# Sink's logit as one more score column in sliding-window attention: one maximum over four heads, negation on ScalarE

## The chip, the cores and the metric

The kernel runs on one core of one Trainium2 chip. Its time is the device time of one execution in microseconds (us). Five engines work side by side, each through its own queue in order: PE (TensorE, matmuls and transposes), DVE (VectorE), ACT (ScalarE), POOL (GpSimd) and SP, which only issues DMAs. "Span" is the time from the first to the last instruction of the profiled execution. Lines such as L1671 are lines of the kernel before; the change shifts what lies behind it (L1671 becomes L1674, L1681 to L1685 become one less or vanish, the later lines are one less).

## The reference

Two transformer blocks run one after the other in fp32: a first block with causal differential attention, stick-breaking attention, cross attention and an MLP, and a second block with sliding-window attention, RWKV and gated linear attention. The change touches only the sliding-window attention. Eight query heads share two key heads (four each), a block has 128 queries, its keys are its own 128 and the 128 before, and each head has a sink: a learned logit that takes part in the softmax and has no value row.

```python
s = jnp.einsum('bnqhgd,bnkhd->bnhgqk', qb, kb) * (D ** -0.5)
s = s - slopes[...] * dist
s = jnp.where(valid[None, :, None, None], s, -jnp.inf)
sink = jnp.broadcast_to(sinks.reshape(Hkv, G)[:, :, None, None], s.shape[:-1] + (1,))
p = jax.nn.softmax(jnp.concatenate([s, sink], axis=-1), axis=-1)[..., :-1]
o = jnp.einsum('bnhgqk,bnkhd->bnqhgd', p, vb)
```

## The kernel before

The sequence of 1024 is worked in two halves of 512 (c = 0 and 1). A weight matmul in fp32 is three matmuls on operands split into a high and a low half (L208 to L210); ACT makes the high half (L200), DVE or POOL the low one (L201).

The sliding attention runs once for each half, in two stretches of the program, called **window 1** (c = 0, g_window0, about 1925 to 2010 us in the profile) and **window 2** (c = 1, in g_tail, about 2230 to 2300 us). Each has 8 units: 4 blocks of 128 queries by 2 key heads. A unit is four heads and has three stages:

- `a()`: eight score matmuls (L1667, L1668) into two PSUM tiles of two heads; for each tile DVE scales it, adds the bias (L1670) and reduces it to its maximum (L1671); then DVE takes the maximum with the sink (L1673), subtracts it from the sink (L1674) and negates it (L1675); ACT takes exp of the sink's difference (L1676) and of each head's scores with their sum (L1678); DVE adds the two (L1681) and takes the reciprocal (L1682); ACT scales heads 0 and 1 (L1684), POOL heads 2 and 3 (L1685).
- `tr()`: PE transposes the probabilities (L1699), ACT copies them out of PSUM (L1702).
- `pv()`: PE multiplies them with the values (L1709), DVE multiplies with the gate (L1711).

The stages of one unit are issued 0, 2 and 3 units late, so that three units are in flight; the scores' tile `wp` has three buffers. The first two units of window 1 have only 128 keys.

Window 1 is woven with the RWKV preparation (g_p2a: projections on PE, elementwise work L1463 to L1549 on DVE, whose result RK goes to DRAM at L1552 and comes back as rk at L1769). Window 2 is woven with the output projection of the rows done (the matmuls on `ya`) and with the first half's final norm (g_final0: loads hd and zd, DVE L2314 and L2316, POOL L2317, store). Behind window 2 come the remaining output projection on `yw` and the last norm. The order on each engine is set by a scheduler that places instructions by estimated durations, so an edit moves neighbours too.

Of the kernel before, what the change touches and what calls it, by code (L numbers as in the profile page):

```python
# [12 lines left out]
F32 = mybir.dt.float32  # L13
# [3 lines left out]
AF = mybir.ActivationFunctionType  # L17
ALU = mybir.AluOpType
AX = mybir.AxisListType
# [3 lines left out]
P = 128  # L23
# [3 lines left out]
CH = 512  # L27
# [141 lines left out]
class K:  # L169
# [1418 lines left out]
    def win_load(s, mx, c):  # L1588

        nc = s.nc  # L1590
        st = [mx.tile([P, 2, CH], F32, tag="wp", name=s.nm("ws"), bufs=3) for _ in range(3)]
        t = [st[i // 2][:, i % 2, :] for i in range(6)]
        sink = mx.tile([P, 8], F32, name="sink")
        s.nc.sync.dma_start(sink, s.A["sink"])
        kst = [mx.tile([P, P + CH], F32R, name=s.nm("k2")) for _ in range(4)]
        q8 = s.tl(s.xp, [P, KT, CH], "act", F32R)
        if c == 1:
            s.nc.sync.dma_start(t[5][:, :P], s.pd[s.AK * P : (s.AK + 1) * P, c * CH - P : c * CH])
        s.get_rows(t[4], s.pd, s.AK, c)
        for h in range(4):  # L1600
            s.get_rows(t[h], s.pd, s.AQ + h, c)
        yield 0
        if c == 1:
            s.stack_k(mx, t[5][:, :P], [k[:, :P] for k in kst])
        s.stack_k(mx, t[4], [k[:, P:] for k in kst])
        yield 0
        qst = []
        for h in range(4):
            qst.append(s.stack_q(mx, t[h], [q8[:, 2 * h, :], q8[:, 2 * h + 1, :]]))
            yield 0  # L1610
        s.win = mx, sink, kst, qst
# [33 lines left out]
    def w_units(s, wn, c, qst, kst, bias, sink, one):  # L1645

        nc = s.nc
        V = nc.vector
        mm = nc.tensor.matmul
        st = {"n": 0}  # L1650

        def unit(b, g):
            u = {}
            nk = 1 if b == 0 else 2
            w = nk * P
# [2 lines left out]
            ga = slice(64 * g, 64 * g + 64)  # L1658

            def a():  # L1660
                p = u["p"] = wn.tile([P, 4, 2 * P], F32, tag="wp", name=s.nm("wp"), bufs=3)
                t = s.sm.tile([P, 6, 4], F32, tag="wt", name=s.nm("wt"))
                for z in range(2):
                    ps = s.ps([P, 2, 2 * P])
                    for y in range(2):
                        q = qst[2 * z + y][g][:, (b % 4) * P : (b % 4 + 1) * P]
                        mm(ps[:, y, :w], q, kst[g][:, k0 : k0 + w], start=True, stop=False)  # L1667
                        mm(ps[:, y, :w], q, kst[2 + g][:, k0 : k0 + w], start=False, stop=True)  # L1668
                    pz = p[:, 2 * z : 2 * z + 2, :w]
                    V.scalar_tensor_tensor(pz, ps[:, :, :w], 0.125, bs[:, 2 * z : 2 * z + 2, :], ALU.mult, ALU.add)  # L1670
                    V.tensor_reduce(t[:, 0, 2 * z : 2 * z + 2], pz, AX.X, ALU.max)  # L1671
                sk = sink[:, 4 * g : 4 * g + 4]
                V.tensor_tensor(t[:, 1, :], t[:, 0, :], sk, ALU.max)  # L1673
                V.tensor_tensor(t[:, 2, :], sk, t[:, 1, :], ALU.subtract)  # L1674
                V.tensor_scalar(t[:, 1, :], t[:, 1, :], -1.0, None, ALU.mult)  # L1675
                nc.scalar.activation(t[:, 2, :], t[:, 2, :], AF.Exp)  # L1676
                for h in range(4):
                    nc.scalar.activation(  # L1678
                        p[:, h, :w], p[:, h, :w], AF.Exp, bias=t[:, 1, h : h + 1], accum_out=t[:, 3, h : h + 1]
                    )  # L1680
                V.tensor_tensor(t[:, 3, :], t[:, 3, :], t[:, 2, :], ALU.add)  # L1681
                V.reciprocal(t[:, 4, :], t[:, 3, :])  # L1682
                for h in range(2):
                    nc.scalar.activation(p[:, h, :w], p[:, h, :w], AF.Copy, scale=t[:, 4, h : h + 1])  # L1684
# [739 lines left out]
```

## Time and profile before

| | us |
|---|---|
| median of 3 runs (lowest, highest) | 2347.19 (2345.37, 2354.68) |
| the profiled execution | 2346.06 |
| its span | 2344.3 |
| PE busy | 2245.4 (96%) |
| DVE busy | 1292.4 (55%) |
| ACT busy | 1034.7 (44%) |
| POOL busy | 691.2 (29%) |

The profiled execution lasts 1.76 us longer than its span, and lies 1.13 us under the median. The shares are means over the whole program; the two windows take about 155 us of it, and there the shares are others: they are in the rows further down. In the rows a form such as 128x4 is partitions by elements, "x8" is how many instructions, "idle before" what the engine stood still ahead of them and for whom.

### The profile page before, as it was taken

Reading aid. Unit: us, or ns where it says so; the run is one execution under the profiler, and the core shown is the slowest. Engines: PE = TensorE matmul, PEld = TensorE weight load, DVE = VectorE, ACT = ScalarE, POOL = GpSimd, SP = SyncE. Lnnn points to the kernel's source line nnn. Section 1 sums busy time; section 2 is a strip of 40 time slices with the busy share of each in tenths; the row PEclk is TensorE's granted clock in tenths of the full one; section 3 lists DMA queues with packets and bytes.
Section 4 is the critical chain, followed back from the end, with each engine's and each line's share of the span. In section 5 each row is a group of like instructions: output and inputs, shape, how many; then the busy total and the mean of one; then the engine's idle time right before and its main releaser. Section 6 shows DMA issues by size and latency. Waiting matters only on the chain.

```text
span 2344.3 us, 34760 instructions
## 1 busy us (share of the span) xinstructions
PE 2245.4 (96%) x13056; PEld 1898.0 (81%) x13056; DVE 1292.4 (55%) x2312; ACT 1034.7 (44%) x2196; POOL 691.2 (29%) x1035
## 2 busy tenths in 40 slices
PE   8999999999999999999999999999999999989886
PEld 7898999988898888888888888887787776677765
DVE  7665656676754554422423422346846658656485
ACT  6655656674643424411311311344633348434463
POOL 4101100000500003556565650035322333224343
PEclk9999999999999999999999999999998999989898
DMA  4010010123241211222222221133343233533461
GB/s 135 28 42 23 31 39 28 46 77 124 66 140 54 99 37 45 75 79 72 77 83 72 78 74 45 52 124 122 119 134 105 74 127 100 166 126 105 131 208 50
DMA packets 116393, 200.06 MB, mean 85 GB/s; under 512 B 14048, under 2 KB 33792, under 8 KB 115456
## 3 DMA queue, kind: packets, MB, share of 16 engines
q1 hardware_dynamic: 111456, 184.72, 24.1%
q0 software_dynamic: 4768, 13.11, 1.7%
q8 instruction: 102, 1.67, 0.3%
q14 instruction: 67, 0.55, 0.1%
HBM read 163.70 MB, written 34.08 MB: 84 GB/s over the span
## 4 chain that ended last, share of the span: by engine, by line
PE 56%; DVE 8%; DMA 4%; ACT 2%; issue 2%; POOL 1%; SPq 0%; DVEq 0%; ACTq 0%; POOLq 0%
PE ps L208 17%; PE ps L209 16%; PE ps L210 16%; DVE act L1957 1%; DVE itmp L1954 1%; PE ps L1827 1%; PE ps L2124 1%; PE ps L1709 1%; DMA stg<-w2l 0%; PE ps L1785 0%; DVE wh L201 0%; DMA stg<-w2t 0%; PE ps L232 0%; DVE wp L1670 0%; ACT wh L200 0%
## 5 line engine op out<-in xcount | busy, mean ns | idle before, releaser
L208 PE MATMUL ps<-act,wh 128*128 128x512 f32 x1664 | 670.3, 405 | 7.5 <-ACT wh L200 5.7
L210 PE MATMUL ps<-act,wh 128*128 128x512 f32 x1664 | 658.1, 396 | 0.0
L209 PE MATMUL ps<-act,wh 128*128 128x512 f32 x1480 | 584.1, 395 | 2.6 <-DVE act L204 1.6
L200 ACT ACTIVATE wh<-stg 128x512 fp32r<-128x512 f32 x374 | 234.6, 630 | 581.4 <-PE ps L209 463.6
L208 PEld LDWEIGHTS ps<-act,wh 128*128 128x128 f32 x1664 | 318.9, 192 | 79.6 <-issue 6.1
L210 PEld LDWEIGHTS ps<-act,wh 128*128 128x128 f32 x1664 | 318.1, 191 | 68.7 <-issue 0.2
L209 PEld LDWEIGHTS ps<-act,wh 128*128 128x128 f32 x1480 | 282.1, 191 | 60.3 <-DVE act L204 2.4
L201 DVE TENSOR_TENSOR wh<-stg,wh 128x512 fp32r<-128x512 f32 x260 | 198.8, 767 | 154.4 <-ACT wh L200 152.9
L201 POOL TENSOR_TENSOR wh<-stg,wh 128x512 fp32r<-128x512 f32 x114 | 161.4, 1420 | 336.3 <-ACT wh L200 301.6
L907 DVE TENSOR_TENSOR act<-ps,act 128x512 f32<-128x512 f32 x112 | 77.0, 689 | 178.0 <-PE ps L210 177.8
L546 DVE TENSOR_TENSOR_SCAN pw<-pw,zero 128x128 f32<-128x128 f32 (+7 forms) x64 | 86.8, 1358 | 82.9 <-POOL pw L542 78.1
L247 POOL TENSOR_TENSOR nacc<-nacc,t 128x512 f32<-128x512 f32 x28 | 39.0, 1396 | 260.4 <-ACT t L246 256.0
L944 POOL TENSOR_TENSOR ad<-ad,cb 128x256 f32<-128x256 f32 x96 | 72.3, 754 | 146.6 <-DMA ad<-adaT 143.6
L1144 DVE SCALAR_TENSOR_TENSOR t<-ps,Rm 128x512 f32<-128x512 f32 x64 | 44.0, 691 | 127.6 <-PE ps L210 126.9
L949 POOL TENSOR_TENSOR ad<-ad 128x128 f32<-128x128 f32 (+5 forms) x288 | 97.3, 338 | 16.8
L208 PE MATMUL ps<-hid,wh 128*128 128x512 f32 x256 | 101.2, 395 | 0.0
L210 PE MATMUL ps<-hid,wh 128*128 128x512 f32 x256 | 101.1, 395 | 0.0
L209 PE MATMUL ps<-hid,wh 128*128 128x512 f32 x256 | 101.0, 395 | 0.0
L1145 ACT ACTIVATE t<-t 128x512 f32<-128x512 f32 x64 | 40.4, 631 | 135.8 <-DVE t L1144 135.8
L208 PE MATMUL ps<-wh,act 128*128 128x256 f32 x320 | 95.9, 300 | 0.0
L210 PE MATMUL ps<-wh,act 128*128 128x256 f32 x320 | 91.3, 285 | 0.0
L209 PE MATMUL ps<-wh,act 128*128 128x256 f32 x320 | 91.1, 285 | 0.0
(515 smaller groups left out, 4663.8 us busy)
## 6 DMA issues: line engine op xcount, KB each, us to landing
stg<-w2f SPq DMA_DIRECT2D x84, 256.0 KB, 3.1
stg<-w_dn SPq DMA_DIRECT2D x80, 256.0 KB, 2.8
stg<-w_up SPq DMA_DIRECT2D x64, 256.0 KB, 2.8
ad<-adaT POOLq DMA_DIRECT2D x96, 128.0 KB, 2.6
stg<-w2o SPq DMA_DIRECT2D x32, 256.0 KB, 2.7
pd<-t SPq DMA_DIRECT2D x30, 256.0 KB, 2.3
t<-yd SPq DMA_DIRECT2D x26, 256.0 KB, 3.5
rkd<-RK SPq DMA_DIRECT2D x4, 1280.0 KB, 5.7
```

What stands on the lines that cost most here:

```text
L200: nc.scalar.activation(hi, src, AF.Copy)
L201: (eng or nc.vector).tensor_tensor(lo, src, hi.bitcast(F32), ALU.subtract)
L208: mm(out, lh, rh, start=first, stop=False)
L209: mm(out, lh, rl, start=False, stop=False)
L210: mm(out, ll, rh, start=False, stop=last)
L247: nc.gpsimd.tensor_tensor(acc, acc, t[:, :n], ALU.add)
L546: V.tensor_tensor_scan(m[:, :w][:, ::-1], m[:, :w][:, ::-1], s.zero.to_broadcast([P, w]), 1.0, ALU.mult, ALU.add)
L907: s.nc.vector.tensor_tensor(hh, ps, hh, ALU.add)
L944: tt(t, t, cb[:, 256 * y : 256 * y + 256], ALU.mult)
L949: tt(acc[:, n, z, :] if w == 2 else a, a, b, ALU.add)
L1144: V.scalar_tensor_tensor(t, ps, 0.0, R[:, c * CH : (c + 1) * CH], ALU.max, ALU.mult)
L1145: nc.scalar.activation(t, t, AF.Square)
```

## The change

The scores' tile gets one more column for each head (4 x 257 instead of 4 x 256). POOL copies the four sinks into column w (128 x 4 elements) at the start of the unit. One reduction over 4 x (w+1) replaces two over 2 x w, and gives the maximum with the sink in it. ACT negates it. Exp runs over w+1 columns, and its sum holds the sink's term. The maximum with the sink, the subtraction, the negation and the addition on DVE go, and so does the Exp of the sink on ACT. The tiles in which the loads are staged have the same tag and take the new size.

```diff
     def win_load(s, mx, c):
-        st = [mx.tile([P, 2, CH], F32, tag="wp", name=s.nm("ws"), bufs=3) for _ in range(3)]
-        t = [st[i // 2][:, i % 2, :] for i in range(6)]
+        st = [mx.tile([P, 4, 2 * P + 1], F32, tag="wp", name=s.nm("ws"), bufs=3) for _ in range(3)]
+        st = [x.rearrange("p a w -> p (a w)") for x in st]
+        t = [st[i // 2][:, i % 2 * CH : i % 2 * CH + CH] for i in range(6)]
...
             def a():
-                p = u["p"] = wn.tile([P, 4, 2 * P], F32, tag="wp", name=s.nm("wp"), bufs=3)
+                p = u["p"] = wn.tile([P, 4, 2 * P + 1], F32, tag="wp", name=s.nm("wp"), bufs=3)
                 t = s.sm.tile([P, 6, 4], F32, tag="wt", name=s.nm("wt"))
+                nc.gpsimd.tensor_copy(p[:, :, w : w + 1], sink[:, 4 * g : 4 * g + 4, None])
                 for z in range(2):
...
                     V.scalar_tensor_tensor(pz, ps[:, :, :w], 0.125, bs[:, 2 * z : 2 * z + 2, :], ALU.mult, ALU.add)
-                    V.tensor_reduce(t[:, 0, 2 * z : 2 * z + 2], pz, AX.X, ALU.max)
-                sk = sink[:, 4 * g : 4 * g + 4]
-                V.tensor_tensor(t[:, 1, :], t[:, 0, :], sk, ALU.max)
-                V.tensor_tensor(t[:, 2, :], sk, t[:, 1, :], ALU.subtract)
-                V.tensor_scalar(t[:, 1, :], t[:, 1, :], -1.0, None, ALU.mult)
-                nc.scalar.activation(t[:, 2, :], t[:, 2, :], AF.Exp)
+                V.tensor_reduce(t[:, 0, :], p[:, :, : w + 1], AX.X, ALU.max)
+                nc.scalar.activation(t[:, 1, :], t[:, 0, :], AF.Copy, scale=-1.0)
                 for h in range(4):
                     nc.scalar.activation(
-                        p[:, h, :w], p[:, h, :w], AF.Exp, bias=t[:, 1, h : h + 1], accum_out=t[:, 3, h : h + 1]
+                        p[:, h, : w + 1], p[:, h, : w + 1], AF.Exp, bias=t[:, 1, h : h + 1],
+                        accum_out=t[:, 3, h : h + 1],
                     )
-                V.tensor_tensor(t[:, 3, :], t[:, 3, :], t[:, 2, :], ALU.add)
                 V.reciprocal(t[:, 4, :], t[:, 3, :])
```

How it moves instructions is shown at three places, each before and after the change. The first is DVE in window 2, the seventh unit (wp_21241 and wt_21242 before, wp_21185 and wt_21186 after), with the neighbours between its scores and the next unit's; before:

```order
L1670 SCALAR_TENSOR_TENSOR wp_21241<-ps_21243,act_18780 128x512
L1670 SCALAR_TENSOR_TENSOR wp_21241<-ps_21250,act_18780 128x512
L1671 TENSOR_REDUCE wt_21242<-wp_21241 128x2 x2
L1681 TENSOR_TENSOR wt_21160<-wt_21160 128x4
L201 TENSOR_TENSOR yw<-t_3766_21055,yw 128x4x128
L1673 TENSOR_TENSOR wt_21242<-wt_21242,sink 128x4
L1682 RECIPROCAL wt_21160<-wt_21160 128x4
L2316 SCALAR_TENSOR_TENSOR t_3804_21275<-t_3804_21275,GP,zacc 128x512
L1674 TENSOR_TENSOR wt_21242<-sink,wt_21242 128x4
L1675 TENSOR_SCALAR wt_21242<-wt_21242 128x4
```

and after, up to the next unit's scores (wp_21246):

```order
L1673 SCALAR_TENSOR_TENSOR wp_21185<-ps_21194,act_18748 128x2x256
L1674 TENSOR_REDUCE wt_21186<-wp_21185 128x4
L2313 SCALAR_TENSOR_TENSOR t_3805_21222<-t_3805_21222,gv,rst 128x512
L201 TENSOR_TENSOR yw<-t_3766_21007,yw 128x4x128
L1710 SCALAR_TENSOR_TENSOR t_3796_21168<-ps_21230,t_3796_21168 64x512
L1673 SCALAR_TENSOR_TENSOR wp_21246<-ps_21249,act_18748 128x2x256
L1673 SCALAR_TENSOR_TENSOR wp_21246<-ps_21255,act_18748 128x2x256
L1681 RECIPROCAL wt_21186<-wt_21186 128x4
```

Before, four instructions of other work (L1681 and L1682 of the sixth unit, L201, L2316) and three steps of the unit's own stand between its second score tile and the negation that ACT's Exp waits for; after, only the reduction does, and the unit's next DVE instruction is its reciprocal, four to five instructions further on.

The second place is POOL in window 1, around the scaling of units 2 and 3 (wh are low halves of weights); before:

```order
L1685 TENSOR_TENSOR wp_18102<-wp_18102,wt_18103 128x2x128
L201 TENSOR_TENSOR wh_18321<-stg_18318,wh_18320 128x512
L1685 TENSOR_TENSOR wp_18183<-wp_18183,wt_18184 128x512
L201 TENSOR_TENSOR wh_18417<-stg_18414,wh_18416 128x512
L201 TENSOR_TENSOR wh_18423<-stg_18420,wh_18422 128x512
L1685 TENSOR_TENSOR wp_18271<-wp_18271,wt_18272 128x512
```

and after:

```order
L1684 TENSOR_TENSOR wp_18098<-wp_18098,wt_18099 128x2x128
L201 TENSOR_TENSOR wh_18225<-stg_18222,wh_18224 128x512
L1665 COPY wp_18259<-sink 128x4
L201 TENSOR_TENSOR wh_18299<-stg_18296,wh_18298 128x512
L1684 TENSOR_TENSOR wp_18175<-wp_18175,wt_18176 128x2x256
L201 TENSOR_TENSOR wh_18305<-stg_18302,wh_18304 128x512
L1665 COPY wp_18350<-sink 128x4
```

The sink's copy stands among the low halves and the scalings; from the fourth unit of a window on it waits for PE's transposes of the unit that held the tile before, and what stands behind it on POOL waits with it. Here wp_18259 is the fourth unit's tile and wp_18350 the fifth's.

The third place is PE in window 2, ahead of the seventh unit's scores (L208 to L210 are the fill matmuls on ya, L1699 the fifth unit's transposes, L1709 the fourth's values); before:

```order
L209 MATMUL ps_21203<-ya_20717,wh_21132 128x512
L210 MATMUL ps_21203<-ya_20717,wh_21133 128x512
L1709 MATMUL ps_21218<-act_18780,vt 128x512 x2
L1699 MATMUL ps_21226<-ident,wp_21069 128x128
L1699 MATMUL ps_21232<-ident,wp_21069 128x128
L1667 MATMUL ps_21243<-k_3670_20536,act_20540 128x256
L1668 MATMUL ps_21243<-k_3672_20538,act_20540 128x256
```

and after:

```order
L209 MATMUL ps_21147<-ya_20685,wh_21080 128x512
L210 MATMUL ps_21147<-ya_20685,wh_21081 128x512
L1708 MATMUL ps_21162<-act_18748,vt 128x512
L1698 MATMUL ps_21170<-ident,wp_21021 128x128 x2
L1698 MATMUL ps_21176<-ident,wp_21021 128x128 x2
L1670 MATMUL ps_21188<-k_3670_20504,act_20508 128x256
```

The last fill matmul stands ahead of the seventh unit's scores before and after, so that the last two units and the drain behind them have none; after, one of the fourth unit's two value matmuls has moved behind the seventh unit's first scores, and two more transposes ahead of them.

## Rows read from the trace of the kernel before

**Rows 1.** The page: the chain that ended last, shares of the span by engine

```profile
PE 56%; DVE 8%; DMA 4%; ACT 2%; issue 2%; POOL 1%; SPq 0%; DVEq 0%; ACTq 0%; POOLq 0%
```

**Rows 2.** Busy time of each engine and PE's clock, in stretches of both windows

```profile
1935.00:1945.00 10.00, 7.63 (x30) 5.89 (x30) 9.40 (x22) 7.24 (x19) 3.79 (x3) 0.83 0.15 51
1975.00:2005.00 30.00, 24.87 (x103) 16.80 (x103) 21.83 (x42) 21.46 (x55) 9.55 (x7) 0.94 0.41 135
2250.00:2300.00 50.00, 37.50 (x172) 24.64 (x171) 42.12 (x76) 32.40 (x93) 18.17 (x14) 0.97 0.57 189
```

**Rows 3.** What PE waited for in window 1: us in total, times, longest

```profile
PE ps L1699 <- ACT wp L1684: 4.6, 2, 2.4
```

**Rows 4.** What PE waited for in window 2

```profile
PE ps L1709 <- ACT act L1702: 8.5, 6, 3.7
PE ps L1699 <- ACT wp L1684: 3.8, 3, 1.6
```

**Rows 5.** DVE's groups in window 1: busy us, mean ns, idle before

```profile
L1671 DVE TENSOR_REDUCE wt<-wp 128x2 f32<-128x512 f32 x12 | 7.8, 672 | 0.0
...
L1675 DVE TENSOR_SCALAR wt<-wt 128x4 f32<-128x4 f32 x8 | 5.0, 629 | 0.1
...
L1681 DVE TENSOR_TENSOR wt<-wt 128x4 f32<-128x4 f32 x8 | 3.4, 431 | 6.9 <-ACT wp L1678 6.9
L1673 DVE TENSOR_TENSOR wt<-wt,sink 128x4 f32<-128x4 f32 x8 | 3.0, 371 | 0.0
...
L1674 DVE TENSOR_TENSOR wt<-sink,wt 128x4 f32<-128x4 f32 x8 | 2.1, 261 | 0.1
```

**Rows 6.** DVE's groups in window 2

```profile
L1675 DVE TENSOR_SCALAR wt<-wt 128x4 f32<-128x4 f32 x8 | 5.9, 733 | 0.2
L1673 DVE TENSOR_TENSOR wt<-wt,sink 128x4 f32<-128x4 f32 x8 | 4.8, 606 | 0.0
...
L1674 DVE TENSOR_TENSOR wt<-sink,wt 128x4 f32<-128x4 f32 x8 | 3.5, 438 | 0.1
L1681 DVE TENSOR_TENSOR wt<-wt 128x4 f32<-128x4 f32 x8 | 3.2, 405 | 1.8 <-ACT wp L1678 1.8
```

**Rows 7.** ACT's groups in window 1

```profile
L1678 ACT ACTIVATE wp<-wp,wt 128x256 f32<-128x256 f32 x24 | 11.9, 495 | 2.3 <-DVE wt L1675 2.3
...
L1676 ACT ACTIVATE wt<-wt 128x4 f32<-128x4 f32 x8 | 1.6, 202 | 3.5 <-DVE wt L1674 3.5
```

**Rows 8.** ACT's groups in window 2

```profile
L1678 ACT ACTIVATE wp<-wp,wt 128x256 f32<-128x256 f32 x32 | 15.9, 497 | 5.2 <-DVE wt L1675 5.1
...
L1676 ACT ACTIVATE wt<-wt 128x4 f32<-128x4 f32 x8 | 1.6, 199 | 3.9 <-DVE wt L1674 3.9
```

**Rows 9.** DVE in order of time, window 1: start, duration

```profile
1939.02 0.68 DVE L1540 TENSOR_TENSOR RK<-pt,pt 128x512 f32<-128x512 f32 x1
1939.62 1.23 DVE L1673 TENSOR_TENSOR wt<-wt,sink 128x4 f32<-128x4 f32 x1
```

**Rows 10.** POOL at the same time

```profile
1938.39 2.44 POOL L201 TENSOR_TENSOR wh<-stg,wh 128x512 fp32r<-128x512 f32 x1 [4.77 <-ACT wh L200]
```

**Rows 11.** DVE in order of time, window 2

```profile
2266.80 1.52 DVE L2316 SCALAR_TENSOR_TENSOR t<-t,GP,zacc 128x512 f32<-128x512 f32 x1
```

**Rows 12.** POOL's smallest groups, whole span

```profile
L949 POOL TENSOR_TENSOR ad<-ad 128x4 f32<-128x4 f32 x48 | 15.5, 323 | 0.7
...
L537 POOL MEMSET pw<- 128x1 f32 x64 | 6.3, 99 | 119.6 <-PE ps L482 119.4
```

**Rows 13.** POOL's low halves of weights in window 1

```profile
L201 POOL TENSOR_TENSOR wh<-stg,wh 128x512 fp32r<-128x512 f32 x15 | 21.9, 1463 | 47.7 <-ACT wh L200 36.7 <-DMA rk<-rkd 9.7 <-PE ps L1490 1.4
```

**Rows 14.** SP's queue, window 1: the store of RK

```profile
1994.27 0.45 SPq L1552 DMA_DIRECT2D rkd<-RK  x1
```

**Rows 15.** POOL behind the load that follows it

```profile
2008.92 1.26 POOL L201 TENSOR_TENSOR wh<-stg,wh 128x512 fp32r<-128x512 f32 x1 [9.66 <-DMA rk<-rkd]
```

**Rows 16.** The chain in order of time, window 2

```profile
2272.32 3.98 DMA t<-hd
```

## The prediction

> **What bounds the kernel now.** I read the chain that ended last first, and in it its shares by engine [rows 1]: PE holds 56%, DVE 8%, everything else little. The kernel as a whole is a matmul kernel, and an edit of some DVE instructions can only pay where PE stands still for them. So the second view is the busy time of the engines in stretches of the two windows [rows 2]. PE is not full there: it is busy 7.63 of 10 us (1935 to 1945), 24.87 of 30 (1975 to 2005) and 37.50 of 50 (2250 to 2300), so it idles 2.37 + 5.13 = 7.50 us in window 1 and 12.50 us in window 2. DVE is the full engine beside it: 9.40 of 10, and 42.12 of 50; in 1975 to 2005 its 21.83 lie nearly all in the first 20 us, since the RWKV work has ended by then. The third view is the waits of PE: in window 1 its transposes wait 4.6 us for ACT's scaling [rows 3], in window 2 its value matmuls wait 8.5 us for ACT's copy of the transposes, and the transposes 3.8 us for the scaling [rows 4]. ACT is named, but ACT itself waits: before the Exps for DVE's negation, 2.3 us in window 1 and 5.1 in window 2, and before the sink's Exp for the subtraction, 3.5 and 3.9 us [rows 7, 8]. That chain (scores, maximum, three small DVE steps, Exp, addition, reciprocal, scaling, transposes, values) is what the windows are bound by, where the DVE steps stand in a queue with RWKV's or the final norm's work.
>
> **What goes from DVE.** Four instructions of 128x4 in each of 16 units. They should be short, and are not: in window 1 the four groups take 5.0 + 3.4 + 3.0 + 2.1 = 13.5 us [rows 5], in window 2 5.9 + 4.8 + 3.5 + 3.2 = 17.4 us [rows 6], 30.9 us together for 64 instructions. The reason is seen in two rows of the same moment: L1673 starts at 1939.62 and lasts 1.23 us to 1940.85 [rows 9], while POOL works on a low half from 1938.39 for 2.44 us, to 1940.83 [rows 10]. The small instruction ends when POOL's does. The wide L1540 ahead of it kept its 0.68 us [rows 9], and POOL's 2.44 us stand against a mean of 1.463 in its group [rows 13]: there POOL waited. I take it that the two engines hold each other off, so that the small steps are worth their stretched times as long as nothing else takes their place.
>
> **What changes in the reductions.** Two reductions of 128x512 cost 2 x 0.672 = 1.34 us [rows 5]. One over 1028 elements costs 0.672 x 1028 / 512 = 1.35 us if all of it goes by the element, and less by one start if not. A start is not shown by itself; the least stretched group of small steps, L1674 at 0.261 us [rows 5], is an upper bound for it. So the saving is 0 to 0.26 us a unit; I take 0.1, which is 1.6 us over 16 units. On the other side the one reduction begins only after the second score tile, where before the first could begin earlier; since DVE is full it has other work meanwhile, and I cost that at nothing; with DVE empty it would be up to 0.67 us a unit.
>
> **What comes to ACT.** The negation takes the place of the sink's Exp: the same form, 0.20 us [rows 7, 8], one for one. The Exps grow by one column of 256, 0.497 / 256 = 0.002 us each, 64 of them: 0.1 us. That an odd width of 257 costs more than its one element, no row shows; the bound on that side is one more small ACT instruction for each Exp, 64 x 0.20 = 13 us of ACT, half hidden since ACT is busy only 32.40 of 50 and 21.46 of 30 us [rows 2]. I take nothing, as the row it is nearest to is the Exp itself. What counts more is the order: the negation now follows the reduction at once on another engine, so that ACT's waits of 2.3 + 3.5 = 5.8 us in window 1 and 5.1 + 3.9 = 9.0 us in window 2 [rows 7, 8] should largely go.
>
> **What comes to POOL.** One copy of 128x4 a unit. Its cost is between a memset of 128x1 at 0.099 and a two-operand step of 128x4 at 0.323 us [rows 12]; with one operand I take 0.2, which is 1.6 us a window. POOL is busy 9.55 of 30 and 18.17 of 50 us [rows 2], so its time is hidden. Its wait is another thing: the first three copies of a window wait for the loads' staging tiles, the later five for PE's transposes of the unit three before, and behind them in POOL's order are low halves of weights and the scalings of heads 2 and 3. These transposes are issued before the scores that need the tile in any case, so most copies will find the tile free. In return DVE's reduction waits for the copy, and behind that reduction stands everything on DVE. I put 1 us on each window for this.
>
> **The sum.** Window 1: of PE's 7.5 us idle, ACT's 5.8 us of waiting is the part that this chain makes. That it also shortens the program needs what ends the window to come earlier. RK's store is issued at 1994.27 [rows 14], and the low halves that PE's next projections want stand behind the load of rk, for which POOL waits 9.66 us until 2008.92 [rows 15]. RK is made on DVE, which is full up to there, and loses 13.5 us of work less what lies behind 1994; so it comes earlier by about as much as PE's idle allows. I take 5.8 + 0.8 (reductions) - 1 = 5.6 us. Window 2: ACT's 9.0 us, but here the chain runs through the final norm's transfers: hd's load of 3.98 us at 2272.32 [rows 16], into a tile that an output store has to leave first. A faster DVE meets that load sooner and then waits for it, with all that is queued behind L2314. I take half of 9.0, and again 0.8 - 1: 4.3, say 4 us. Together 9.6, rounded down to 9 us since some of the moved neighbours will fall badly. The profiled execution would go from 2346.06 to 2337; it lies 1.13 us under the median, so the median goes from 2347.19 to **2338**. The bounds: nothing at all from window 2 and half of window 1 gives 3 us; both windows with ACT's whole waits give 14.8. So 2332 to 2344 is the forecast's own range.
>
> A rule of the Trainium skill speaks against counting the stretched times. SBUF — State Buffer, section "SBUF: two separate sides", says that VectorE and GpSimd share one pair of ports under an exclusive lock: a VectorE instruction with two operands in SBUF (or in a two-port mode) and a GpSimd instruction exclude each other for their whole length, and whichever starts first wins. The trace agrees with the exclusion (1.23 us for L1673 [rows 9]). By this rule the stretch isn't a property of the small steps: the next DVE instruction that needs the pair inherits it. That is the second rival.
>
> **Rivals.**
> First, all of the idle time goes: DVE was the sole bound, and PE fills its 7.50 and 12.50 us. For it: PE at a mean granted clock of 0.83 in 1935 to 1945 [rows 2], a mixture of its levels of 1.2 and 2.4 GHz in a stretch in which it stood still, so that a stall also costs speed behind it. Against it: the last two units of window 2 have no fill matmuls in either order, and idle time there is the latency of the chain. 2347 - 20 = 2327.
>
> Second, the stretches are handed on. L2316 took 1.52 us at 2266.80 [rows 11], a wide two-operand step with POOL at work: so wide steps can be stretched too. Then the gain is the small steps' own time, at most 64 x 0.261 = 16.7 instead of 30.9 us, and the sum shrinks in proportion to 9 x 16.7 / 30.9 = 4.9 us; the copies, at most 16 x 0.323 = 5.2 us of POOL, stretch others in turn and take about half of that. Against it: in window 1 most instructions that follow the small ones read PSUM or are reductions. About -2 us, 2345.
>
> Third, slower: the copy at the head of POOL's queue. The place is the five later units of each window, ten copies; the price is a DVE queue that stands at its reduction until POOL has come past a low half whose high half ACT has not made. POOL waited 36.7 us for ACT ahead of 15 low halves [rows 13], 2.4 us each; ten times that is 24 us. Less the 9 us won it is +15 us, 2362. It decides from the fourth such wait on (4 x 2.4 exceeds the 9 us). For it: the copies stand between low halves in POOL's new order. Against it: the copies can run as soon as the tile is free, which is a unit ahead of the reduction.
>
> **Chances and range.** Forecast 0.50, all idle gone 0.15, handed on 0.24, slower through POOL 0.11. A measurement of this kernel can tell about 0.5% from no change, 11.7 us. Faster by more than that is the first rival, 0.15, and the forecast's far end, 0.13: 0.28. Slower by more is most of the third, 0.08. Within is the rest, 0.64. The range of 8 in 10 goes from 2328, which takes in most of the first rival, to 2350, which takes in the handing-on and an extra wait or two, and leaves out the third.
>
> **What would show it.** Right: DVE's busy time falls by some 30 us in the two windows, ACT's waits ahead of the Exps shrink to under 1 us a window, and PE's idle in the three stretches falls from 20.0 to about 11 us, with nothing moved elsewhere. The handing-on would show as longer means of L2314, L2316, L201 and RWKV's two-operand steps; the load as a DVE wait for hd well over what it is now; the third rival as DVE's reduction waiting for POOL's copy. The forecast is wrong if the windows end when they did although DVE has less to do, or if a wait of DVE for POOL of several us stands in them.

## The result and the profile after

The changed kernel took 2336.29 us (median of 12 runs, 2329.39 to 2343.58) against 2351.80 us for the kernel before (12 runs, 2345.37 to 2357.62): a ratio of 0.9939, 95% interval 0.9923 to 0.9955, so 14.3 us faster (10.6 to 18.1) by the ratio. The forecast was 9 us faster, 2338 us. The profiled execution took 2335.09 us with a span of 2333.3 us, 11.0 us less than before.

Where did the 11.0 us of this pair go? I cut both traces at the same instructions: window 1 from its first score matmul to the first transpose of rk behind its last scores, window 2 from its first score matmul to the end of its last value matmul.

| stretch | before, us | after, us |
|---|---|---|
| ahead of window 1 | 1922.6 | 1919.1 |
| window 1 | 87.4 | 85.0 |
| between | 211.8 | 209.1 |
| window 2 | 79.8 | 76.4 |
| behind | 42.7 | 43.6 |

Only 5.8 us lie in the two windows. What lies ahead of window 1 is the same program in all kernels of this study but for the first copies of the sink, and its length went from 1917.0 to 1925.3 us over their 14 traces, whichever arithmetic followed; so one pair of traces can't apportion the gain, and below I use means over several.

**The clock beside the times.** The record lists each run of the experiments with the mean clock that TensorE was granted. Of 29 runs of the kernel before, the slowest (2357.91 us) had 0.967 and the fastest (2336.56 us) 0.975, and over all 29 a straight line falls by 1.7 us for each 0.001 of clock. The traces show it too: ahead of window 1 the clock stood at the lower of its two levels (0.50, 1.2 GHz) for 41.0 us in the trace of dummy_steps (1917.1 us long there) and for 64.9 us in that of add_dve (1925.0 us); over the 14 traces the two go together with a correlation of 0.84. So two kernels should also be compared at the same clock. Two parallel straight lines of time against clock, through the runs of a kernel and those of the kernel before beside it, give that difference, with a standard error of 0.8 to 1.2 us; it is the last column of the table further down. For the first comparison the clocks of the kernel before aren't on record; the changed kernel run again (after_again) is 11.3 us faster at the same clock.

The clock isn't chance alone. In window 1 of the kernel before PE stood still for 2.37 us:

```profile
1941.49 0.48 PE L1699 MATMUL ps<-ident,wp 128*128 128x128 f32 x1 [2.37 <-ACT wp L1684]
```

and the clock read 0.50 from 1941.1 on, for 3.4 us (columns as in [rows 2]):

```profile
1941.10:1944.50 3.40, 3.01 (x12) 2.82 (x13) 2.80 (x7) 3.37 (x6) 0.77 (x2) 0.50 0.22 77
```

All five kernels that keep the small steps on the chain in window 1 stood still at this place, for 2.4 to 3.8 us, and in four of them the lower level followed, for 3.4 or 6.8 us (not in w2_only). None of the other nine has the lower level in this half of the window, though neg_dve stands still there for 3.5 us. After the change the three stretches of [rows 2] read:

```profile
1935.00:1945.00 10.00, 7.83 (x39) 5.95 (x38) 9.37 (x19) 9.91 (x24) 4.73 (x5) 1.00 0.24 74
1975.00:2005.00 30.00, 26.48 (x109) 17.66 (x107) 17.35 (x27) 17.67 (x41) 8.90 (x7) 0.94 0.55 181
2250.00:2300.00 50.00, 43.28 (x236) 32.84 (x235) 41.17 (x61) 32.95 (x93) 18.79 (x19) 0.93 0.47 153
```

So a part of the gain in window 1 goes through the clock, and the comparison at the same clock leaves that part out: 3.4 us at the lower level are 0.0007 of the mean clock, some 1.2 us on the line.

The instructions themselves came out as costed. This is DVE's reduction in window 1 after the change, for the six units with 256 keys (columns as in [rows 5]):

```profile
L1674 DVE TENSOR_REDUCE wt<-wp 128x4 f32<-128x1028 f32 x6 | 7.3, 1218 | 0.1
```

ACT's groups of window 2 [rows 8]:

```profile
L1677 ACT ACTIVATE wp<-wp,wt 128x257 f32<-128x257 f32 x32 | 15.9, 499 | 0.4
...
L1675 ACT ACTIVATE wt<-wt 128x4 f32<-128x4 f32 x8 | 1.6, 197 | 4.3 <-DVE wt L1674 4.3
```

and the sink's copy over the whole span (duration in ns: least, median, largest):

```profile
L1665 POOL COPY wp<-sink x16: 187/192/705, 1906.8 to 2268.3; 128x4 f32<-128x4 f32 x16
```

One reduction takes 1.218 us where two took 1.344 (I took 0.1 us off, it is 0.13); the negation 0.20 us; an Exp over 257 columns 0.499 us against 0.497; the copy 0.19 us in the middle (I took 0.2). ACT's wait ahead of the Exps in window 2 is gone (0.4 us against 5.2), and what waiting there is now stands at the negation, for the reduction.

PE's waits in window 2, from 2220 to 2300 us, as in [rows 4]:

```profile
PE ps L1708 <- ACT act L1701: 5.3, 5, 2.9
PE ps L208 <- ACT ya L200: 3.6, 1, 3.6
PE ps L1670 <- DVE wp L1673: 0.9, 1, 0.9
PE ps L1698 <- POOL wp L1684: 0.5, 1, 0.5
```

The value matmuls wait 5.3 instead of 8.5 us, and the transposes' 3.8 us behind ACT's scaling are gone. In window 1 the transposes wait 0.8 instead of 4.6 us [rows 3], and the value matmuls more than before (2.9 us):

```profile
PE ps L1708 <- ACT act L1701: 5.1, 2, 3.5
PE ps L1698 <- ACT wp L1683: 0.8, 1, 0.8
```

**The unit's chain.** The next view is DVE and ACT in order of time. The eighth and last unit of window 2 before the change, on DVE:

```profile
2285.82 1.29 DVE L1670 SCALAR_TENSOR_TENSOR wp<-ps,act 128x512 f32<-128x512 f32 x2
2287.03 0.68 DVE L1671 TENSOR_REDUCE wt<-wp 128x2 f32<-128x512 f32 x1
2287.62 0.15 DVE L1681 TENSOR_TENSOR wt<-wt 128x4 f32<-128x4 f32 x1
2287.69 0.75 DVE L2314 SCALAR_TENSOR_TENSOR t<-t,gv,rst 128x512 f32<-128x512 f32 x1
2288.35 0.68 DVE L1671 TENSOR_REDUCE wt<-wp 128x2 f32<-128x512 f32 x1
2288.95 0.17 DVE L1682 RECIPROCAL wt<-wt 128x4 f32<-128x4 f32 x1
2289.03 0.72 DVE L2316 SCALAR_TENSOR_TENSOR t<-t,GP,zacc 128x512 f32<-128x512 f32 x1
2289.67 1.02 DVE L1673 TENSOR_TENSOR wt<-wt,sink 128x4 f32<-128x4 f32 x1
2290.73 0.69 DVE L1711 SCALAR_TENSOR_TENSOR t<-ps,t 64x512 f32<-64x512 f32 x1
2291.45 0.47 DVE L1674 TENSOR_TENSOR wt<-sink,wt 128x4 f32<-128x4 f32 x1
2291.95 0.17 DVE L1675 TENSOR_SCALAR wt<-wt 128x4 f32<-128x4 f32 x1
```

and its first Exp on ACT:

```profile
2292.56 0.50 ACT L1678 ACTIVATE wp<-wp,wt 128x256 f32<-128x256 f32 x1
```

The second score tile is done at 2287.11 and the first Exp starts at 2292.56: 5.45 us, of which the three small steps themselves take 1.66 us, and L2314, L1682, L2316 and L1711, which belong to others and stand in between, 2.33 us (with L1681 of the unit before, 2.48 us). The sixth unit after the change, on DVE:

```profile
2266.47 0.68 DVE L1673 SCALAR_TENSOR_TENSOR wp<-ps,act 128x512 f32<-128x512 f32 x1
2267.18 1.22 DVE L1674 TENSOR_REDUCE wt<-wp 128x4 f32<-128x1028 f32 x1
```

and on ACT:

```profile
2268.43 0.20 ACT L1675 ACTIVATE wt<-wt 128x4 f32<-128x4 f32 x1 [3.51 <-DVE wt L1674]
2268.73 0.51 ACT L1677 ACTIVATE wp<-wp,wt 128x257 f32<-128x257 f32 x1
```

From 2267.15 to 2268.73 it is 1.58 us. These are two single units: over the eight units of window 2 this time is 5.83 us before and 2.42 us after in the mean, over those of window 1 6.28 and 3.10 us. The whole chain was worked out for every unit in the same way. The mean over a window's eight units, from the end of the second score tile to the end of the reciprocal (four Exps of about 2.0 us in it):

| kernel | chain in window 1, us | chain in window 2, us | ratio | us against before, at the same clock |
|---|---|---|---|---|
| before | 10.53 | 10.70 | 1 | 0 |
| pad257 | 10.87 | 11.24 | 1.0005 | -0.5 |
| neg_act_only | 9.92 | 10.61 | 1.0031 | +2.5 |
| before_red | 9.89 | 10.38 | 0.9980 | -5.3 |
| w1_only | 6.01 | 11.08 | 0.9958 | -5.2 |
| w2_only | 10.67 | 5.47 | 0.9953 | -5.8 |
| dummy_steps | 6.10 | 6.67 | 0.9968 | -8.1 |
| dummy_red | 5.89 | 6.15 | 0.9962 | -9.3 |
| neg_dve | 5.53 | 7.40 | 0.9952 | -8.7 |
| add_dve | 5.87 | 6.35 | 0.9952 | -12.5 |
| dummy_recip | 5.65 | 5.97 | 0.9937 | -11.5 |
| copy_act | 5.77 | 5.73 | 0.9944 | -12.1 |
| after_again | 6.01 | 5.75 | 0.9947 | -11.3 |
| after | 6.01 | 5.78 | 0.9939 | not on record |

The other kernels are those of the next section. The ratios fall into two groups: 0.998 and more where the chain is about 10 us in both windows, 0.997 and less where it is about 6 in one or both, and a kernel with one short window comes out like one with two. At the same clock one short window gives 5 to 6 us and two give 8 to 12.5 us. before_red stands outside: 5.3 us with a chain that is hardly shorter.

The chain isn't the only thing that goes this way. The edit makes the scheduler order PE's work anew: in window 1, 43 of PE's 351 instructions stand in another place after the change. Every kernel with a long chain there has the order of the kernel before but for 9 instructions at most, and every one with a short chain that of the changed kernel but for 10 at most. What the new order would be worth with the long chain, or the short chain in the old order, no run shows.

### The profile page after: what moved, and what is told of

The parts are those of the page before. It is cut to its first block, busy times and chain, and to the rows that moved or that the text cites. A ratio compares the mean times of both kernels' runs of the same rounds, so it can differ in the third digit from the quotient of the medians.

```text
span 2333.3 us, 34698 instructions
## 1 busy us (share of the span) xinstructions
PE 2236.6 (96%) x13056; PEld 1894.1 (81%) x13056; DVE 1275.9 (55%) x2232; ACT 1033.8 (44%) x2196; POOL 693.9 (30%) x1051
## 4 chain that ended last, share of the span: by engine, by line
PE 79%; DVE 9%; ACT 4%; DMA 4%; issue 3%; POOL 1%; SPq 0%; DVEq 0%; POOLq 0%; ACTq 0%
PE ps L208 21%; PE ps L209 21%; PE ps L210 21%; PE ps L561 2%; PE ps L482 2%; DVE act L1956 1%; DVE itmp L1953 1%; PE ps L468 1%; PE ps L469 1%; PE ps L699 1%; PE ps L1708 1%; PE ps L1826 1%; DMA stg<-w2l 1%; DVE wh L201 1%; ACT pw L675 1%
## 5 line engine op out<-in xcount | busy, mean ns | idle before, releaser
L208 PE MATMUL ps<-act,wh 128*128 128x512 f32 x1664 | 666.2, 403 | 7.7 <-ACT wh L200 5.7
L210 PE MATMUL ps<-act,wh 128*128 128x512 f32 x1664 | 658.6, 396 | 0.4 <-POOL wh L201 0.4
L208 PEld LDWEIGHTS ps<-act,wh 128*128 128x128 f32 x1664 | 317.6, 191 | 78.9 <-issue 5.7
L210 PEld LDWEIGHTS ps<-act,wh 128*128 128x128 f32 x1664 | 317.4, 191 | 68.7 <-POOL wh L201 0.8
L201 DVE TENSOR_TENSOR wh<-stg,wh 128x512 fp32r<-128x512 f32 x260 | 199.8, 771 | 156.0 <-ACT wh L200 153.7
L201 POOL TENSOR_TENSOR wh<-stg,wh 128x512 fp32r<-128x512 f32 x114 | 160.3, 1411 | 303.1 <-ACT wh L200 278.4
L546 DVE TENSOR_TENSOR_SCAN pw<-pw,zero 128x128 f32<-128x128 f32 (+7 forms) x64 | 86.8, 1358 | 83.8 <-POOL pw L542 79.1
L208 PE MATMUL ps<-hid,wh 128*128 128x512 f32 x256 | 101.3, 396 | 0.0
L210 PE MATMUL ps<-hid,wh 128*128 128x512 f32 x256 | 101.2, 395 | 0.0
L208 PE MATMUL ps<-wh,act 128*128 128x256 f32 x320 | 95.5, 299 | 0.0
L210 PE MATMUL ps<-wh,act 128*128 128x256 f32 x320 | 91.0, 284 | 0.0
```

The source lines that it names most:

```text
L201: (eng or nc.vector).tensor_tensor(lo, src, hi.bitcast(F32), ALU.subtract)
L208: mm(out, lh, rh, start=first, stop=False)
L210: mm(out, ll, rh, start=False, stop=last)
L546: V.tensor_tensor_scan(m[:, :w][:, ::-1], m[:, :w][:, ::-1], s.zero.to_broadcast([P, w]), 1.0, ALU.mult, ALU.add)
```

## The experiments

Ratios are against the kernel before, run on the same chip, with their 95% interval; an amount in us is the ratio applied to some 2350 us. Two theories stand against each other. Latency: the gain comes from the shorter chain, that is from places in DVE's queue that a unit no longer passes. DVE time: it comes from the 30.9 us of small steps, stretched by POOL [rows 5, 6], that DVE no longer does.

**The change again, and each window alone.** after_again is the changed kernel; w1_only and w2_only take the new arithmetic and the wider tile where c is 0, or 1, and the old elsewhere:

```diff
+                if c == 0:
+                    nc.gpsimd.tensor_copy(p[:, :, w : w + 1], sink[:, 4 * g : 4 * g + 4, None])
...
+                if c == 0:
+                    V.tensor_reduce(t[:, 0, :], p[:, :, : w + 1], AX.X, ALU.max)
```

> The changed kernel once more, as a yardstick for its parts and for the stretches ahead of window 1, which are instruction for instruction those of before. If the gain is the change's own, about -14 us (ratio 0.994), and the time to the last activation load ahead of window 1 (1896.3 us before, 1892.9 after) scatters by some us either way. If a good part of the gain is chance of executions, the ratio comes nearer to the 6.6 us that the two windows show in the traces (0.997).

> The change in window 1 alone, window 2 as before. My sum put 5.6 us on window 1; the two traces show the stretch from 1919 to 2012 us shorter by 2.3 us only. If the traces hold, -2 to -4 us. Rival: both windows give half of the measured 14 us, then -7 us. Second rival: window 1 gives nothing, since the load of rk sets its end, then 0.

> The change in window 2 alone, window 1 as before. My sum put 4 us on window 2, since the final norm's loads would take the rest; the two traces show the stretch from 2232 to 2300 us shorter by 4.3 us. If the traces hold, -4 to -6 us. Rival: half of the measured 14 us, -7 us; if the loads of hd set the pace, -1 us or less.

Measured: again 0.9947 (0.9927 to 0.9967), window 1 alone 0.9958 (0.9939 to 0.9976), window 2 alone 0.9953 (0.9936 to 0.9969): 12, 10 and 11 us faster. The gain is the change's own. By the ratios the halves are each larger than any expectation and add up to more than the whole. The clock accounts for that: both halves ran at a mean clock of 0.9724, the kernel before at 0.9695 and the whole change at 0.9697. At the same clock window 1 alone gives 5.2 us and window 2 alone 5.8 us (standard errors 1.1 and 1.0), together 11.0, and the whole change 11.3 us. The traces can split the gain too, since w1_only has the order of the changed kernel up to window 2 and w2_only that of the kernel before. Window 1 is 87.4, 87.4 and 87.8 us with the old arithmetic in that order (before, w2_only, and pad257 below), and 85.0, 83.3, 83.8 and 80.3 us with the new (after, after_again, w1_only, and add_dve below, which has the changed kernel's order up to window 2): means of 87.5 and 83.1, so 4.4 us. Window 2 is 79.8, 84.9 and 85.3 us with the old (before, w1_only, pad257), and 76.4, 77.6 and 73.6 with the new (after, after_again, w2_only): means of 83.3 and 75.9, so 7.5 us. Together 11.9 us, inside the interval of the timing. But three or four traces a side leave some 3 us each way on the first difference and 6 us on the second, and the time at the lower level of the clock differs as well: in window 1 5.7 us with the old arithmetic against 1.7 with the new, in window 2 13.7 against 10.2 us, in the mean.

**Small steps put back, off the chain.** dummy_steps keeps the new arithmetic and adds four unused steps; dummy_recip and dummy_red add four reciprocals or four reductions in their places. The edit of dummy_steps:

```diff
                 nc.scalar.activation(t[:, 1, :], t[:, 0, :], AF.Copy, scale=-1.0)
+                V.tensor_tensor(t[:, 2, :], t[:, 0, :], sink[:, 4 * g : 4 * g + 4], ALU.max)
+                V.tensor_tensor(t[:, 5, :], sink[:, 4 * g : 4 * g + 4], t[:, 2, :], ALU.subtract)
+                V.tensor_scalar(t[:, 2, :], t[:, 2, :], -1.0, None, ALU.mult)
...
+                V.tensor_tensor(t[:, 5, :], t[:, 5, :], t[:, 2, :], ALU.add)
                 V.reciprocal(t[:, 4, :], t[:, 3, :])
```

> The changed kernel with four small DVE steps of 128x4 put back into each unit, on the same kinds of operands (maximum with the sink, subtraction, negation, addition), whose results nobody uses. If the gain is the chain's latency (negation right behind the maximum, no DVE step between Exp and reciprocal), it keeps most of the gain: -9 us or better. If the gain is DVE's time, stretched by POOL as in the kernel before, the steps cost the 30.9 us of DVE again and the gain is gone: within 3 us of before.

> The changed kernel with four reciprocals of 128x4 put into each unit where dummy_steps had its four small steps, results unused. A reciprocal never lasted beyond 0.18 us in any trace here, so it adds about 0.17 us of DVE each, at most 11 us over 64, but no stretch. If the stretch behind POOL is what the small steps cost, the gain stays: window 1 near 84 us, -11 us or better in all. If it is their number and place in DVE's queue, it comes out as dummy_steps did: window 1 near 87.5 us and about -7 us.

> dummy_steps with its four unused steps turned into reductions of 128x4: the same order on every engine, so that only the stretch differs. dummy_steps kept about half of the gain (-7.5 us, window 1 at 87.5 us), four reciprocals kept all (-14.6, 79.8) but in an order of their own. If the stretch makes the difference: -11 us or better and window 1 below 85 us. If the order did it: as dummy_steps, -7 us and 87 us.

Measured: dummy_steps 0.9968 (0.9952 to 0.9985), dummy_recip 0.9937 (0.9919 to 0.9956), dummy_red 0.9962 (0.9947 to 0.9977): 7.5, 14.8 and 8.9 us faster. In dummy_steps the added steps took 9.6 and 10.0 us of DVE in the two windows, and the chain stayed at 6.10 and 6.67 us; half of the gain stayed. That speaks for latency: by DVE time, with 19.6 of 30.9 us back, about 5 us would be left, which the interval doesn't exclude either. At the same clock 8.1 us are left (standard error 0.8), against 4.1 us by the same reckoning from 11.3. dummy_red has dummy_steps' order on every engine, and steps that don't stretch (0.15 us each). Its ratio is the same within the intervals. Its window 1 was 83.7 us against 87.5, but there the clock differed: it stood at the lower level for 6.8 us in the trace of dummy_steps and not at all in that of dummy_red, and PE was busy 80.5 and 77.2 us. dummy_recip kept the whole gain in an order of its own (window 1 79.8 us). I had expected dummy_red to follow it if stretch decides; it didn't. At the same clock the three are 8.1, 9.3 and 11.5 us faster, with standard errors of 0.8 to 0.9; whether the step from the second to the third is order or chance stays open.

**The kernel before without the stretch.** before_red replaces the four small steps where they stand, on the chain, in an order that is that of the kernel before on all engines. It leaves out the sink and the signs, so that only its time is of use:

```diff
-                V.tensor_tensor(t[:, 1, :], t[:, 0, :], sk, ALU.max)
-                V.tensor_tensor(t[:, 2, :], sk, t[:, 1, :], ALU.subtract)
-                V.tensor_scalar(t[:, 1, :], t[:, 1, :], -1.0, None, ALU.mult)
+                V.tensor_reduce(t[:, 1, :], t[:, 0, :, None], AX.X, ALU.max)
+                V.tensor_reduce(t[:, 2, :], t[:, 1, :, None], AX.X, ALU.max)
+                V.tensor_reduce(t[:, 1, :], t[:, 1, :, None], AX.X, ALU.max)
...
-                V.tensor_tensor(t[:, 3, :], t[:, 3, :], t[:, 2, :], ALU.add)
+                V.tensor_reduce(t[:, 3, :], t[:, 3, :, None], AX.X, ALU.max)
```

> The kernel before with its four small DVE steps replaced, one for one and in the same order on every engine, by reductions of 128x4 on the same operands (the sink and the signs are left out of the softmax). Reductions never lasted longer beside POOL here. If the stretch behind POOL is what the steps cost, the small steps fall from 30.9 to about 10 us of DVE and a good part of the gain appears: -5 to -9 us, window 1 at 84 us or less instead of 87.4. If their number and place in the queue is the cost, or the order that the scheduler made: 0 to -2 us, window 1 at 87.

Measured: 0.9980 (0.9963 to 0.9998), 4.7 us faster. Its DVE groups in window 1:

```profile
L1681 DVE TENSOR_REDUCE wt<-wt 128x4 f32<-128x4 f32 x8 | 1.2, 152 | 6.3 <-ACT wp L1678 6.3
L1675 DVE TENSOR_REDUCE wt<-wt 128x4 f32<-128x4 f32 x8 | 1.2, 152 | 0.1
L1673 DVE TENSOR_REDUCE wt<-wt 128x4 f32<-128x4 f32 x8 | 1.2, 148 | 0.0
L1674 DVE TENSOR_REDUCE wt<-wt 128x4 f32<-128x4 f32 x8 | 1.2, 145 | 0.1
```

The small steps fell from 13.5 to 4.8 us there, and DVE's busy time in the window from 63.0 to 56.3 us, less than the changed kernel's 58.9. The window before the change, in this run and after the change (columns as in [rows 2]):

```profile
1922.58:2009.98 87.40, 79.89 (x351) 57.11 (x350) 62.97 (x141) 58.22 (x147) 30.01 (x24) 0.96 0.46 148
1925.32:2012.45 87.13, 80.68 (x351) 58.39 (x350) 56.32 (x141) 58.81 (x147) 30.17 (x24) 0.94 0.45 149
1919.14:2004.17 85.03, 79.03 (x354) 56.42 (x353) 58.91 (x103) 58.39 (x148) 30.66 (x30) 0.98 0.49 156
```

Yet the window lasted 87.1 us, and the chain 9.89 us: the unit still passes the same places in DVE's queue. This is the run that tells the theories apart best. With less DVE time in window 1 than the changed kernel, and without the shorter chain, it is worth a third of the gain by the ratio (0.5 to 8.7 us of 14.3), and 5.3 of 11.3 us at the same clock (standard error 0.8). So neither theory holds alone: DVE's shorter time is worth something by itself, and the larger half, some 6 us (a difference of two figures with errors near 1 us each), comes with the shorter chain, or with the new order that came with it. In its window 1 nothing is seen of the 5.3 us, but there the clock stood at the lower level for 10.2 us, against 6.8 in the kernel before.

**Parts of the change.** neg_dve is the changed kernel with DVE's negation, neg_act_only the kernel before with ACT's. The edit of neg_dve:

```diff
-                nc.scalar.activation(t[:, 1, :], t[:, 0, :], AF.Copy, scale=-1.0)
+                V.tensor_scalar(t[:, 1, :], t[:, 0, :], -1.0, None, ALU.mult)
```

> The changed kernel with the negation on DVE instead of ACT (one small step of 128x4 in each unit, 0.15 us or stretched to 1.3). If ACT's negation, right behind the reduction, carries the gain: -5 us or less is left. If it is one of four steps and no more than that, a quarter is lost: -10 us. If the place of the negation is indifferent (ACT waits for the same reduction either way): -13 us, as the whole change.

> The kernel before with only the negation moved to ACT, behind the sink's Exp: two reductions, maximum, subtraction and addition stay on DVE, no extra column. If each small step counts by its time, 10.9 of 30.9 us go from DVE and with them a third of the gain: -4 to -5 us. If the stretch only moves on to the next step that needs it: 0 to -2 us. If ACT's wait for the negation was what held the chain: -8 us.

Measured: neg_dve 0.9952 (0.9937 to 0.9967), 11 us faster: which engine negates is worth some 3 us, also at the same clock (8.7 against 11.3 us), and nothing for certain. neg_act_only was 1.0031 (1.0018 to 1.0044), 7 us slower, which no theory had. Its small steps' time fell (4.0 + 2.7 + 1.3 = 8.0 us instead of 13.5 in window 1), but its chain stayed at 9.92 and 10.61 us, so by latency no gain was due; and the stretch between the windows took 219.0 us, where all others took 208.3 to 215.1. There PE stood still at a place that in the kernel before had no stall:

```profile
2090.36 6.87 PE L1827 MATMUL ps<-AV,act 64*64 64x128 f32 x31 [3.99 <-ACT act L1982]
```

On ACT the copy of L1982 stood behind a high half that waited for a load:

```profile
2087.81 1.37 ACT L200 ACTIVATE act<-t 128x512 fp32r<-128x512 f32 x2 [3.88 <-DMA t<-yd]
2089.09 0.61 ACT L200 ACTIVATE wh<-stg 128x512 fp32r<-128x512 f32 x1
2089.72 1.06 ACT L1982 ACTIVATE act<-ps 32x512 f32<-32x512 f32 x2
```

and the same 31 matmuls took 3.60 us in the kernel before, at a clock of 1.00. Here they ran at the lower level (columns as in [rows 2]):

```profile
2090.36:2097.20 6.84, 6.84 (x34) 6.84 (x35) 1.02 (x2) 3.19 (x6) 1.94 (x2) 0.50 0.36 117
```

The edit had moved some instructions and loads there through the scheduler, though it touches none of them. The runs had a mean clock of 0.9664 against 0.9690; at the same clock 2.5 of the 7 us are left (standard error 1.2), and that this place alone makes them was not tested.

**The copy's engine, the width, and a try at more.** copy_act copies the sink's column on ACT; pad257 is the kernel before with the wider tile, its last column unused, in the same order; add_dve is the changed kernel with the final norm's addition on DVE:

```diff
-                nc.gpsimd.tensor_copy(p[:, :, w : w + 1], sink[:, 4 * g : 4 * g + 4, None])
+                nc.scalar.activation(p[:, :, w : w + 1], sink[:, 4 * g : 4 * g + 4, None], AF.Copy)
...
-            nc.gpsimd.tensor_tensor(z, z, h, ALU.add)
+            V.tensor_tensor(z, z, h, ALU.add)
```

> The changed kernel with the sink's column copied by ACT instead of POOL (0.2 us of ACT a unit). If the copy in POOL's queue costs nothing, as the traces say (POOL's wait for PE ahead of it is 2.6 us in all), the time stays at -13 us or loses up to 2 us for ACT's 3.2 us. If the copy holds up low halves or the reduction, it gains 2 to 4 us more.

> The kernel before with the scores' tile 257 wide for each head and the last column unused; the order on every engine is that of before. If the odd stride costs nothing, 0 us, within the interval of the comparison, which at the same time shows what it can tell apart. If reading at a stride of 1028 bytes costs ACT or DVE anything, +1 to +5 us.

> The changed kernel with the final norm's addition in window 2 (L2316) on DVE instead of POOL: eight POOL instructions of 1.39 us go, DVE gets eight of 0.68 us, and the stretched wide steps of window 2 (wb 1.16, wh 0.89, L2313 1.01 us) should come back to 0.68 to 0.75. If the handed-on stretch still costs the window, -2 to -4 us against the change, -15 us or better against before. If DVE's own time counts as much, no difference from the change; if window 2 hangs on the loads of hd, no difference either.

Measured: copy_act 0.9944 (0.9928 to 0.9960), so POOL's queue was no burden. pad257 1.0005 (0.9991 to 1.0020): the odd stride costs nothing that can be measured. add_dve 0.9952 (0.9934 to 0.9971): no better than the change, though eight POOL instructions went: L2313 and the wh halves came back to 0.77 and 0.68 us as expected, wb still took 0.94 us and yw 1.14. No version beat the change for certain.

## Why the prediction was right, point by point

- **The bound.** Right as far as the runs go: the windows are bound by what a unit does between its scores and its values, much of it in DVE's queue. How the gain divides between shorter chain, less DVE time and new order, they don't settle. PE's idle time in window 1 fell from 8.0 to 5.1 us (means of the old and the new runs named above), in window 2 from 15.6 to 11.1; that is 7.4 of the 11.9 us by the windows. The rest is shorter busy time of PE, part of it the clock's.
- **What goes from DVE.** The 30.9 us went, but they aren't worth their stretched times: some 12 us came back elsewhere (second rival). before_red shows the stretch alone at 4.7 us (0.5 to 8.7), 5.3 us at the same clock. The rest comes with three of DVE's steps no longer standing between the score tile and the Exp, and one fewer behind it: 4.5 to 4.9 us of chain a unit.
- **Reductions, ACT, POOL.** Sizes right, as read above. The copies' wait that I put 1 us on a window for was 2.2 us of POOL's time in window 1 and 0.4 in window 2, and DVE idled 0.1 and 0.2 us ahead of the reductions: it cost nothing that shows.
- **The sum.** Window 1: 5.6 us forecast, 5.2 measured by w1_only at the same clock (4.4 between the traces). Window 2: 4 us forecast, 5.8 measured by w2_only (7.5 between the traces). With standard errors of about 1 us neither term is shown wrong. If one is mis-sized it is the second, in which I took half of ACT's 9.0 us off for the loads of hd. The load did come to meet DVE: its waits for hd and zd rose from 1.3 us to 2.6 + 3.1 us. That the unit whose chain it holds has 4.9 us to give, more than the wait takes, is an argument that no run tests. The gain didn't come by the route that the sum took, and that the sizes fit is partly luck: in window 1 ACT's 5.8 us of waiting were to go, and ACT waits 10.1 us after the change (9.8 at the negation, of which 5.2 stand ahead of the first unit); in window 2 its 9.0 us fell to 4.7. The clock has no term in the sum either. The whole, 11.9 us by the windows and 14.3 by the timing, stands within the range (2328 to 2350); the 9 us of the forecast lie below the interval of the timing (10.6 to 18.1).
- **First rival** (all idle time goes): no; 16 us of idle is left in the two windows. What it said beside that, that a stall also costs speed behind it, is borne out in window 1: the lower level behind the stall at 1939 us is gone with the change.
- **Second rival** (the stretches are handed on): its mechanism is real, its verdict isn't. Wide steps that had taken 0.67 to 0.84 us were stretched after the change; in window 1, RWKV's:

```profile
L1544 DVE TENSOR_TENSOR pt<-pt,pt 128x512 f32<-128x512 f32 x2 | 2.5, 1228 | 0.0
L1533 DVE TENSOR_TENSOR RK<-mix,pt 128x512 f32<-128x512 f32 x2 | 2.4, 1194 | 0.0
L1547 DVE TENSOR_TENSOR RK<-pt,pt 128x512 f32<-128x512 f32 x2 | 2.3, 1173 | 0.0
L1543 DVE SCALAR_TENSOR_TENSOR RK<-pt,pt 128x512 f32<-128x512 f32 x2 | 2.3, 1151 | 0.0
```

  and in window 2:

```profile
L2313 DVE SCALAR_TENSOR_TENSOR t<-t,gv,rst 128x512 f32<-128x512 f32 x8 | 8.0, 1005 | 2.6 <-DMA t<-hd 2.6
...
L201 DVE TENSOR_TENSOR wb<-stg,wb 128x512 fp32r<-128x512 f32 x4 | 4.7, 1164 | 0.1
L201 DVE TENSOR_TENSOR wh<-stg,wh 128x512 fp32r<-128x512 f32 x4 | 3.6, 890 | 0.0
L201 DVE TENSOR_TENSOR yw<-t,yw 128x512 fp32r<-128x512 f32 x3 | 2.8, 947 | 0.6 <-ACT yw L200 0.6
```

  Before, L1544, L1533, L1547 and L1543 took 0.68 us each, wb 0.67, wh 0.68, yw 0.69 and L2314 (now L2313) 0.80. Two of these rows of before:

```profile
L1544 DVE TENSOR_TENSOR pt<-pt,pt 128x512 f32<-128x512 f32 x2 | 1.4, 678 | 0.0
...
L201 DVE TENSOR_TENSOR wb<-stg,wb 128x512 fp32r<-128x512 f32 x4 | 2.7, 668 | 0.0
```

  Summed over the groups of each window, about 6 us in window 1 and 5.5 in window 2 came back this way, some 12 of 30.9 us. My argument against it, that most followers in window 1 read PSUM or are reductions, left these four out, which read SBUF alone; and that the wide L1540 kept its 0.68 us [rows 9] was one instruction that happened to come first. The rule of the Trainium skill (SBUF — State Buffer, "SBUF: two separate sides") is that a VectorE instruction with two inputs in SBUF and a GpSimd instruction that reads SBUF exclude each other. From it the prediction drew that the next one which needs the shared ports inherits the wait, and these rows agree. The gain was well above this rival's 2 us all the same.
- **Third rival** (POOL's queue): no; copy_act shows no difference that can be measured.
- **The markers.** Three failed although the time was right. ACT's waits didn't shrink to under 1 us but moved to the negation (9.8 us in window 1, 4.3 in window 2). DVE's busy time fell by 13.6 us in the windows instead of 30: its durations fell by 20.5 us in sum, since 12 us were handed on, and the records of neighbours overlap (by some 0.08 us in the rows above), so that a small step adds less to the busy time than it lasts. And one pair of traces showed gains outside the windows that are scatter. The fourth nearly held: PE's idle in the three stretches is 12.4 us against the 11 that I gave, in stretches that hold other work after the change.

## What to carry to other kernels

In a queue that is shared by several streams, an instruction on a dependent chain costs the place it waits for beside its duration. Here the same small steps made three times shorter in place brought about half of the gain, and taking them off the chain went with the rest. Measure it as the time from the end of the producer to the start of the consumer, unit by unit, in both traces. Where a scheduler sets the order, compare kernels of the same order (or several of each). And don't read a gain of a few us from one pair of traces: the same program ahead of the change scattered by 8 us, and the granted clock of each run tells much of that. Put the clock beside every time before two halves of a change are added up.

## What the runs showed of the hardware

- Which small DVE steps are stretched beside POOL: 128x4 TENSOR_TENSOR and TENSOR_SCALAR went up to 1.29 us, while 128 reductions of the same size stayed between 0.143 and 0.153 us on average in each group (before_red, dummy_red; the longest took 0.161 us), and reciprocals between 0.155 and 0.179 us in the kernel before, and never over 0.181 us in the others.
- Executions of one and the same program scatter by about as much as the change moves: 2345.37 to 2357.62 us for the kernel before, 2329.39 to 2343.58 us for the changed one, and 8.3 us in the stretch ahead of window 1.
- The scatter goes with TensorE's granted clock: over the 29 runs of the kernel before beside before_red, from 0.967 at 2357.91 us to 0.975 at 2336.56 us, a line falls by 1.7 us for each 0.001. In window 1 of the kernel before the clock read 0.50 for 3.4 us directly behind a stall of PE of 2.37 us, and after the change it read 1.00 there.
